# Seven products for seven of eight up-projection pieces, and adding transfers for half of the down pieces, in a streaming-encoder block

## The chip, the core and the metric

The kernel runs on one core of a Trainium2 chip. The metric is the device time of one execution in microseconds. The core's engines run side by side, each through its own list of instructions in a fixed order, and wait for one another through semaphores: TensorE (PE, matmuls and, as PEld, the loads of their stationary operand), VectorE (DVE), ScalarE (ACT), GpSimd (POOL) and SyncE (SP, which issues most transfers). Data lie in HBM, in the on-chip SBUF, and in PSUM, eight banks of 128 x 512 float32 into which TensorE writes.

## What is computed

One layer of an encoder block on 256 tokens of width 2048: a gated feed-forward, a mixing stage with two recurrences, a cross attention, a second feed-forward, and a last norm. The change touches the two feed-forwards alone:

```
D_MODEL = 2048; SEQ = 256; DEPTH = 1
D_FF = 256 * ((8 * D_MODEL // 3 + 255) // 256)      # 5632

def swiglu(h, w_up, w_down):
    gate, up = jnp.split(h @ w_up, 2, axis=-1)
    return (jax.nn.silu(gate) * up) @ w_down

x = x + 0.5 * swiglu(rms_norm(x, ffn1_norm[l]), ffn1_w_up[l], ffn1_w_down[l])
...
x = x + 0.5 * swiglu(rms_norm(x, ffn2_norm[l]), ffn2_w_up[l], ffn2_w_down[l])
```

All of it is float32.

## The kernel before

**High and low parts.** A float32 operand is split into a high part `h` (a rounded copy, made by ScalarE) and a low part `l` (the remainder, a subtraction on VectorE); `split`, L119 to L121, issues the two. A product is then three matmuls of 128 x 128 by 128 x 512: high by high, low by high, high by low (`three`, L448 to L454). The first loop of `three` issues all matmuls with the weights' high parts, the second those with their low parts.

**Pieces.** Weights come in pieces of 128 x 2048 float32, 1 MB each. The hidden width of 5632 is cut into 11 groups of 512 columns. The up-projection of one group takes eight pieces, p = 0 to 7; a piece holds two blocks of 128 rows of the gate half and of the up half, that is four 128 x 512 blocks, and multiplies a pair of blocks of the activations, for two halves of 128 tokens. That is a 2 x 2 by 2 x 2 block product. It is done in one of three ways, by the table `PRODUCTS`:

- "plain" (first group): 8 products, 24 matmuls.
- "fast": 7 products, 21 matmuls. It is a seven-product scheme which needs differences of weight blocks. `prepare` (L195 to L222) makes them: `td`, four 512-wide blocks by three VectorE instructions (L213 to L215), and then splits 1536 columns of the piece into `h` and `l` and the differences, in two halves, into `th` and `tl`. It also needs sums of activation blocks, which `operand_pairs` makes ahead ("sums", into the second half of the slots `xh` and `xl`).
- "mixed": 8 products, 24 matmuls, that add into the same seven accumulators as the fast ones. It needs the weights' plain `h` and `l` alone, but two differences of activation blocks ("less"), 256 columns.

In the second and third group (g = 1, 2) even p are mixed and odd p fast. From the fourth on (g = 3 to 10) p = 0 and p = 6 are mixed, the six others fast, in the order 1, 3, 0, 4, 2, 6, 5, 7. The seven accumulators take seven of the eight PSUM banks. After the last piece of a group they are combined (`e0` to `e3`, L535 to L547), made into the hidden activations (`activate`, L483 and L484) and, some pieces later, turned by TensorE (`turn`, L491 to L496).

**Down pieces.** The down-projection of a block of 512 hidden columns has four pieces (c = 0 to 3), each 24 matmuls (`three`, for two halves of tokens), all plain. From g = 3 on four down pieces follow every group; the down pieces of two blocks are worked off over two groups, so that c takes one pair of accumulators for two pieces, and after the second the residual is updated (L563). `ffn_order` (L42 to L58) writes the whole order.

**Adding transfers.** `prepare` has a second way to make the low part, the kind "added" (`begin_added`, L186 to L193): the piece is loaded into `own`, a pool of one buffer; ScalarE writes its negative, rounded, into `l`; then a transfer issued by POOL adds `own` to `l`, so that VectorE has no part in it. `prepare` later lets ScalarE write `h` from `own`. This is begun one piece ahead of the others. In the kernel before, both mixed pieces of every group from the fourth on are "added", except p = 0 of the fourth group, which is plain: 15 pieces per feed-forward.

**Order on the engines.** `weights` prepares one piece ahead of the piece that is multiplied. What of this stands where on each engine is then settled by the framework's scheduler when the program is built; the instructions of neighbouring pieces interleave. Buffers: three each for `raw`, `h`, `l`, and for "wide", which holds `td`, `tl` and the combination buffer `ev`; 24 slots of 1024 columns for activations.

**Sums of activations.** In `operand_pairs` the list `BOTH` names the pairs which need both "less" (for the second and third group) and "sums" (from the fourth on): 2 and 4. Their "less" lies in a slot `xd` of its own, two pairs wide; for the other even pairs it lies in the second half of `xh` and `xl`. In the first feed-forward the sums of pairs 2 and 4 are made when pieces 17 and 18 of the plan (counted from 0) are prepared, by the dictionary `rest`.

Of the kernel before, what the change touches and what calls it, by code (L numbers as in the profile page):

```python
# [9 lines left out]
F32R = mybir.dt.float32r  # L10
# [3 lines left out]
P = 128  # L14
# [5 lines left out]
NG = DFF // 512  # L20
# [21 lines left out]
def ffn_order():  # L42

    out, down = [("plain", 0, p) for p in range(8)], [("down", 0, 1, c, 0) for c in range(4)]
    for g in range(1, NG):
        if g < 3:  # L50
            out += [(("mixed", "fast")[p % 2], g, p) for p in (0, 1, 2, 3, 5, 4, 7, 6)]
        else:
            out += [("mixed" if p in (0, 6) else "fast", g, p) for p in (1, 3, 0, 4, 2, 6, 5, 7)]
        if g > 2 and g % 2:
            down = [("down", g - 2, 2, c, b) for c in range(4) for b in (g - 2, g - 1)]
        n = 2 if g < 3 else 4
        out, down = out + down[:n], down[n:]
    return out + [("down", NG - 2, 2, c, b) for c in range(4) for b in (NG - 2, NG - 1)]  # L58
# [3 lines left out]
def block_kernel(ctx: ExitStack, tc: tile.TileContext, xT, xin, memT, vec, gfin, bgate, lruw, wu1, wd1, win, wv,  # L62
# [14 lines left out]
    scoped = {}  # L77

    @contextmanager
    def scope(**pools):  # L80
        with ExitStack() as inner:
            for name, bufs in pools.items():
                scoped[name] = inner.enter_context(tc.tile_pool(name=name, bufs=bufs, reuse_waits="tile"))
            yield
            scoped.clear()

    def slot(dt=F32, name="slot"):
        return slots.tile([P, 1024], dt, name=name, tag="slot")
# [12 lines left out]
    def col(name, i=0, n=1):  # L101
        a = VEC[name][0] + i
        return vt[:, a:a + n]
# [15 lines left out]
    def split(h, l, raw):  # L119
        done["high"] = act.activation(h, raw, ACT.Copy).ins  # L120
        dve.tensor_tensor(out=l, in0=raw, in1=h.bitcast(F32), op=ALU.subtract)  # L121
# [4 lines left out]

    plan, ahead = [], []
    orders = dict.fromkeys(("ffn1", "ffn2"), ffn_order())

    def plan_ffn(name, wu, wd):  # L130
        for e in orders[name]:
            src = wd[e[4], e[3]] if e[0] == "down" else wu[e[1], e[2]]
            kind = "fast" if e[0] == "fast" else "added" if e[0] == "mixed" and e[1:] > (3, 0) else "plain"
            plan.append(((name,) + e, src, kind))

    def plan_columns(name, w, which):
# [2 lines left out]
    def plan_rows(name, w, g):  # L139
        plan.extend(((name, g, kq), w[g, kq], "plain") for kq in range(w.shape[1]))  # L140

    plan_ffn("ffn1", wu1, wd1)
    for hf in range(2):
        for base in (8, 0):
# [11 lines left out]
    for name, w in (("mv", wvm), ("o", wo)):  # L156
        for g in range(4):
            plan_rows(name, w, g)
    plan_ffn("ffn2", wu2, wd2)

    head, rest = [], {}
# [175 lines left out]
            return r  # L337


    FFN_POOLS = dict(wide=3, own=1)  # L340

    class TokenSquares:

# [58 lines left out]

    BOTH = [2, 4]
    xd = []

    def operand_pairs(src, gain, q, xg, out):

        for a in src:  # L410
            i = len(out)
            g = xg[:, i * 512:(i + 1) * 512]
            for z in range(2):
                act.activation(g[:, z * T:][:, :T], a[:, z * T:(z + 1) * T], ACT.Copy,
                               scale=col(gain, 4 * q + 2 * i + z))
            h, l = slot(F32R, "xh"), slot(F32R, "xl")
            split(h[:, :512], l[:, :512], g)
            less = None if i else (h[:, 512:768], l[:, 512:768])
            if 2 * q + i in BOTH:
                if 2 * q + i == BOTH[0]:  # L420
                    xd.append(slot(F32R, "xd"))
                n = 512 * BOTH.index(2 * q + i)
                less = [xd[-1][:, a:a + 256] for a in (n, n + 256)]
            out.append(((h, l), less))

        def sums(which=((0, "less"), (0, "sums"), (1, "less"), (1, "sums"))):
            s = slot(name="xs")
            for i, ((h, l), less) in enumerate(out):
                a = [xg[:, i * 512 + j * P:][:, :P] for j in range(4)]

                def made(h, l, n, at, terms):
                    o = [s[:, at + j * P:][:, :P] for j in range(n)]
                    for j, (x, y, op) in enumerate(terms(o)):
                        dve.tensor_tensor(out=o[j], in0=x, in1=y, op=op)
                    split(h, l, s[:, at:at + n * P])

                if less and (i, "less") in which:
                    made(*less, 2, 0, lambda o: ((a[0], a[1], ALU.subtract), (a[2], a[3], ALU.subtract)))
                if (i or 2 * q in BOTH) and (i, "sums") in which:
                    if not i and len(which) > 1:  # L440
                        s = slot(name="xs")
                    made(h[:, 512:], l[:, 512:], 4, 512 * i,
                         lambda o: ((a[1], a[3], ALU.add), (o[0], a[0], ALU.subtract),
                                    (a[1], a[0], ALU.subtract), (a[2], o[1], ALU.subtract)))

        return sums
# [130 lines left out]
    def head_x(p):  # L577

        q = p // 2
        if p % 2 == 0:  # L580
            xq[q] = slot(name="xf"), slot(name="xg"), []
        src, xg, out = xq[q]
        a = p % 2 * 512
        sp.dma_start(src[:, a:a + 512], xT[:, p * 512:(p + 1) * 512])
        sums = operand_pairs([src[:, a:a + 512]], "ffn1_norm", q, xg, out)
        if p % 2:
            sums1.append(sums)
        pairs1.append(out[-1])
# [19 lines left out]
    made = rest[7], rest[8]  # L608
    rest[7] = lambda: [f() for f in (lambda: head_residual(3), made[0])]
    rest[8] = lambda: [f() for f in (head_rstd, made[1])]  # L610
    for q, i in ((1, 17), (2, 18)):
        rest[i] = lambda q=q: sums1[q](((0, "sums"),))


# [48 lines left out]

    with scope(**FFN_POOLS):
        ffn("ffn1", pairs1, sq1, to_mix, rstds=rstd1)
# [390 lines left out]
    def to_ffn(c):  # L1056
        out = []
        sums2.append(operand_pairs(turned(xt[c]), "ffn2_norm", c, slot(name="xg"), out))
        pairs2.extend(out)
        if c < 2:  # L1060
            sums2.pop(0)()
# [34 lines left out]

    with scope(**FFN_POOLS):
        ffn("ffn2", pairs2, sq4, to_out, late, sums2)
# [93 lines left out]
```

## Time and profile before

| | |
|---|---|
| time, median of 3 runs | 2442.7 us (2442.57 to 2443.22) |
| profiled execution, its own time | 2442.24 us |
| its span, first to last instruction | 2440.5 us |
| mean granted TensorE clock | 0.999 |
| DMA | 507.59 MB, mean 208 GB/s |

How to read it: "busy" is the time that an engine spends in instructions; for a matmul the end is modelled, so matmuls of 0.39 us each that begin 0.23 us apart overlap. A row of a group gives line, engine, operation, tile written, tiles read, shape, count, then busy time and mean nanoseconds of one, then the idle time of the engine before them and what ended it. A row of a timeline gives start and length in microseconds. A row of the waits gives engine and line, what it waited for, the total in us, how often, and the longest. A row of stretches gives from and to, length, busy time (and instructions) of PE, PEld, DVE, ACT and POOL, the granted clock, the busy share of the 16 DMA engines and GB/s.

### The profile page before, as it was taken

How to read it: one execution, taken by the hardware profiler on the slowest of the kernel's cores; microseconds unless marked ns; L12 is line 12 of the kernel's file. 1: busy time of each engine (PE TensorE's matmuls, PEld its weight loads, DVE VectorE, ACT ScalarE, POOL GpSimd, SP SyncE). 2: the span in 40 equal slices, each digit the busy share in tenths (PEclk: the TensorE clock that was granted, in tenths of full speed). 3: DMA queues.
4: the chain of work that ended last, by engine and by line, in shares of the span. 5: the costliest groups of instructions: out<-in, count | busy, mean ns of one | idle time of the engine just before them, and what ended most of it. 6: DMA issues, size and time to landing. Idle time of an engine off the chain costs nothing.

```text
span 2440.5 us, 30183 instructions
## 1 busy us (share of the span) xinstructions
PE 2430.0 (100%) x12250; PEld 2033.8 (83%) x12250; DVE 1892.8 (78%) x2016; ACT 1390.8 (57%) x1398; POOL 28.3 (1%) x36
## 2 busy tenths in 40 slices
PE   9999999999999999999999999999999999999998
PEld 8888888888888888888888888888888888888887
DVE  6999999999765757577565676556589999999995
ACT  8566666666554454477435554555555666666664
POOL 0000000000000000000000000000000000000000
PEclk9999999999999999999999999999999999999999
DMA  8557777677555545445555555544555677777763
GB/s 296 207 204 243 255 234 236 234 241 239 200 181 192 180 173 179 176 171 217 191 189 186 206 196 190 190 173 155 189 191 185 232 238 234 234 239 241 237 216 151
DMA packets 75020, 507.59 MB, mean 208 GB/s; under 512 B 8320, under 2 KB 8576, under 8 KB 15232
## 3 DMA queue, kind: packets, MB, share of 16 engines
q1 hardware_dynamic: 69840, 473.06, 53.3%
q0 software_dynamic: 4320, 31.46, 6.7%
q8 instruction: 96, 1.57, 0.2%
q10 hardware_dynamic: 720, 1.13, 0.1%
q14 instruction: 44, 0.36, 0.0%
HBM read 472.07 MB, written 2.10 MB: 194 GB/s over the span
## 4 chain that ended last, share of the span: by engine, by line
PE 97%; DVE 1%; ACT 1%; DMA 1%; issue 0%; SPq 0%; ACTq 0%; DVEq 0%
PE acc L451 18%; PE acc L454 18%; PE acc L452 18%; PE acc L231 11%; PE acc L252 8%; PE acc L253 8%; PE acc L255 8%; PE acc L235 6%; PE acc L491 1%; PE acc L391 1%; ACT h L120 0%; PE acc L768 0%; DVE l L121 0%; DMA xf<-xT 0%; PE acc L1051 0%; PE acc L1006 0%
## 5 line engine op out<-in xcount | busy, mean ns | idle before, releaser
L121 DVE TENSOR_TENSOR l<-raw,h 128x2048 fp32r<-128x2048 f32 (+2 forms) x422 | 877.9, 2087 | 364.8 <-ACT h L120 354.7
L120 ACT ACTIVATE h<-raw 128x2048 fp32r<-128x2048 f32 (+2 forms) x422 | 736.7, 1752 | 615.1 <-PE acc L253 206.2
L451 PE MATMUL acc<-h,xh 128*128 128x512 f32 x1280 | 499.0, 391 | 0.4 <-ACT h L120 0.3
L452 PE MATMUL acc<-h,xl 128*128 128x512 f32 x1280 | 496.9, 389 | 0.0
L120 ACT ACTIVATE h<-td 128x1024 fp32r<-128x1024 f32 x224 | 229.7, 1056 | 177.0 <-PE acc L452 130.8
L252 PE MATMUL acc<-h,ops 128*128 128x512 f32 x832 | 326.9, 393 | 0.0
L253 PE MATMUL acc<-h,ops 128*128 128x512 f32 x832 | 324.3, 390 | 0.0
L121 DVE TENSOR_TENSOR tl<-td,h 128x1024 fp32r<-128x1024 f32 x224 | 267.4, 1220 | 31.6 <-ACT h L120 29.0
L451 PEld LDWEIGHTS acc<-h,xh 128*128 128x128 f32 x1280 | 240.3, 188 | 53.2 <-ACT h L120 3.4
L452 PEld LDWEIGHTS acc<-h,xl 128*128 128x128 f32 x1280 | 240.3, 188 | 49.4
L231 PE MATMUL acc<-ops,h 128*128 128x512 f32 x1152 | 277.9, 393 | 0.2
L451 PE MATMUL acc<-h,hidop 128*128 128x512 f32 x704 | 275.7, 392 | 0.0
L452 PE MATMUL acc<-h,hidop 128*128 128x512 f32 x704 | 274.3, 390 | 0.0
L231 PEld LDWEIGHTS acc<-ops,h 128*128 128x128 f32 x1152 | 211.9, 188 | 42.8 <-DVE ops L292 0.9
L454 PE MATMUL acc<-l,xh 128*128 128x512 f32 x832 | 218.3, 389 | 0.0
L255 PE MATMUL acc<-l,ops 128*128 128x512 f32 x832 | 206.1, 390 | 0.0
L454 PE MATMUL acc<-l,hidop 128*128 128x512 f32 x704 | 188.3, 389 | 0.0
L255 PEld LDWEIGHTS acc<-l,ops 128*128 128x128 f32 x832 | 156.2, 188 | 32.4
L454 PEld LDWEIGHTS acc<-l,xh 128*128 128x128 f32 x832 | 156.0, 188 | 32.5
L252 PEld LDWEIGHTS acc<-h,ops 128*128 128x128 f32 x832 | 156.3, 188 | 32.3
L253 PEld LDWEIGHTS acc<-h,ops 128*128 128x128 f32 x832 | 156.3, 188 | 31.6
L454 PEld LDWEIGHTS acc<-l,hidop 128*128 128x128 f32 x704 | 132.2, 188 | 27.5
(220 smaller groups left out, 2347.9 us busy)
## 6 DMA issues: line engine op xcount, KB each, us to landing
raw<-wu SPq DMA_DIRECT2D x142, 1024.0 KB, 4.8
raw<-wd SPq DMA_DIRECT2D x88, 1024.0 KB, 4.8
raw<-win SPq DMA_DIRECT2D x40, 1024.0 KB, 4.8
raw<-wg SPq DMA_DIRECT2D x32, 1024.0 KB, 4.8
own<-wu SPq DMA_DIRECT2D x30, 1024.0 KB, 5.4
l<-own POOLq DMA_DIRECT2D x30, 1024.0 KB, 7.7
raw<-wab SPq DMA_DIRECT2D x16, 1024.0 KB, 4.8
raw<-wout SPq DMA_DIRECT2D x16, 1024.0 KB, 4.8
```

The costliest lines, as they stand in the source:

```text
L120: done["high"] = act.activation(h, raw, ACT.Copy).ins
L121: dve.tensor_tensor(out=l, in0=raw, in1=h.bitcast(F32), op=ALU.subtract)
L231: pe.matmul(acc, h[:, k * P:(k + 1) * P], xs[k], start=k == 0, stop=False)
L235: done["product"] = pe.matmul(acc[:, :T], l[:, k * P:(k + 1) * P], xs[k][:, :T], start=False, stop=k == KT - 1).ins
L252: pe.matmul(accs[t], x[:, t * P:][:, :P], h[j], start=first and j == 0, stop=False)
L253: pe.matmul(accs[t], x[:, T + t * P:][:, :P], h[j], start=False, stop=False)
L255: done["product"] = pe.matmul(accs[t], x[:, t * P:][:, :P], l[j], start=False, stop=last and j == 3).ins
L391: pe.transpose(accs[m // 2][:, m % 2 * T + t * P:][:, :P], tile[:, t * 512 + m * P:][:, :P], ident)
L451: pe.matmul(acc, ah, bh, start=start, stop=False)
L452: pe.matmul(acc, al, bh, start=False, stop=False)
L454: pe.matmul(acc, ah, bl, start=False, stop=stop)
L491: pe.transpose(acc[:, z * T + t * P:][:, :P], hid[t][:, (2 * y + z) * P:][:, :P], ident)
```

## The change

From the fourth group on p = 0 becomes fast, so that only p = 6 is mixed, and the order of the pieces becomes 1, 3, 0, 6, 4, 2, 5, 7. The kind "added" now goes to the mixed piece of every group from the fourth on, that of the fourth included, and to every second down piece of the blocks 1 to 8: two of the four that follow each group from g = 3 to g = 10, the first and the fourth of them. `BOTH` gains pair 0. As `xd` has room for two, the "less" of the third pair (4) is put in a buffer of a new pool `third` of 512 columns, made when it is first written. In the first feed-forward the sums of pairs 0, 2 and 4 are made at pieces 22, 23 and 24 of the plan.

```diff
@@ ffn_order
         else:
-            out += [("mixed" if p in (0, 6) else "fast", g, p) for p in (1, 3, 0, 4, 2, 6, 5, 7)]
+            out += [("mixed" if p == 6 else "fast", g, p) for p in (1, 3, 0, 6, 4, 2, 5, 7)]
@@ plan_ffn
-            kind = "fast" if e[0] == "fast" else "added" if e[0] == "mixed" and e[1:] > (3, 0) else "plain"
+            kind = "fast" if e[0] == "fast" else "plain"
+            if e[0] == "mixed" and e[1] > 2:
+                kind = "added"
+            if e[0] == "down" and 0 < e[1] < NG - 2 and (e[3] + e[4] - e[1]) % 2 == 0:
+                kind = "added"
@@
-    FFN_POOLS = dict(wide=3, own=1)
+    FFN_POOLS = dict(wide=3, own=1, third=1)
@@ operand_pairs
-    BOTH = [2, 4]
+    BOTH = [0, 2, 4]
...
-                less = [xd[-1][:, a:a + 256] for a in (n, n + 256)]
+                less = [xd[-1][:, a:a + 256] for a in (n, n + 256)] if n < 1024 else []
...
+                if less == [] and (i, "less") in which:
+                    third = scoped["third"].tile([P, 512], F32R, name="xd", tag="xd")
+                    less.extend((third[:, :256], third[:, 256:]))
@@
-    for q, i in ((1, 17), (2, 18)):
+    for q, i in ((0, 22), (1, 23), (2, 24)):
         rest[i] = lambda q=q: sums1[q](((0, "sums"),))
```

## The prediction

> **What bounds the kernel now.** I read the page's head first, then the waits of TensorE, then busy time by stretch, and last the order of single instructions inside one group.
>
> ```profile
> span 2440.5 us, 30183 instructions
> PE 2430.0 (100%) x12250; PEld 2033.8 (83%) x12250; DVE 1892.8 (78%) x2016; ACT 1390.8 (57%) x1398; POOL 28.3 (1%) x36
> ```
> ```profile
> PE warm L109 <- DVE ones L106: 1.1, 1, 1.1
> PE acc L451 <- ACT h L120: 0.3, 1, 0.3
> ```
> TensorE (PE) is busy all the span and waits 1.4 us in total. Its busy time is modelled, so the second view is needed: nothing holds it up. The two feed-forward stages are therefore as long as their list of matmuls. What could take over is seen by stretch (PE, weight loads, DVE, ACT, POOL, then clock, DMA share, GB/s):
>
> ```profile
> 110.00:172.00 62.00, 62.00 (x282) 51.02 (x281) 60.75 (x59) 35.62 (x31) 0.00 (x0) 1.00 0.51 187
> 1840.00:1902.00 62.00, 62.00 (x282) 50.98 (x281) 57.69 (x56) 36.50 (x31) 0.00 (x0) 1.00 0.54 190
> 2011.40:2073.50 62.10, 62.10 (x279) 51.52 (x278) 57.37 (x56) 38.36 (x32) 1.76 (x2) 1.00 0.72 237
> ```
> The last row is one whole period of a group from the fourth on: PE 62.10 of 62.10, VectorE (DVE) 57.37, so 4.73 us of DVE are free. In the third group of the first feed-forward DVE is at 60.75 of 62.00: there it is nearly the second bound. The granted clock is 1.00 in all three.
>
> **What is removed: 48 matmuls.** In the order of PE's instructions the pieces of one group begin at
>
> ```profile
> 345.67 0.39 PE L451 MATMUL acc<-h,xh 128*128 128x512 f32 x1
> 349.52 1.07 PE L454 MATMUL acc<-tl,xh 128*128 128x512 f32 x4
> 350.43 0.39 PE L451 MATMUL acc<-h,xh 128*128 128x512 f32 x1
> 355.19 0.39 PE L451 MATMUL acc<-h,xh 128*128 128x512 f32 x1
> 360.63 0.39 PE L451 MATMUL acc<-h,xh 128*128 128x512 f32 x1
> ```
> Two "fast" pieces of 7x3 matmuls take 4.76 us each, the "mixed" piece of 8x3 takes 5.44: 0.227 us a matmul. Groups 3 to 10 of two feed-forwards turn one piece each: 16 x 0.68 = 10.9 us. The path it lies on is PE's own, without cover. More than that cannot be gained, since PE waits for nothing that could go away; a period becomes 62.10 - 0.68 = 61.42 us.
>
> **What it adds on DVE.**
>
> ```profile
> 348.74 2.36 DVE L121 TENSOR_TENSOR tl<-td,h 128x1024 fp32r<-128x1024 f32 x2
> 351.01 1.22 DVE L213 TENSOR_TENSOR td<-raw 128x1024 f32<-128x1024 f32 x1
> 357.54 1.22 DVE L213 TENSOR_TENSOR td<-raw 128x1024 f32<-128x1024 f32 x1
> 365.61 1.22 DVE L213 TENSOR_TENSOR td<-raw 128x1024 f32<-128x1024 f32 x1
> 378.29 2.36 DVE L121 TENSOR_TENSOR tl<-td,h 128x1024 fp32r<-128x1024 f32 x2 [0.98 <-ACT h L120]
> 383.86 4.49 DVE L121 TENSOR_TENSOR l<-raw,h 128x2048 fp32r<-128x2048 f32 x2 [0.53 <-ACT h L120]
> 388.27 0.68 DVE L536 TENSOR_TENSOR ev<-acc,ev 128x512 f32<-128x512 f32 x1
> ```
> A fast piece costs DVE 357.54 - 351.01 = 6.53 us; the low part of a plain down piece (388.27 - 383.86)/2 = 2.20. Per group: +6.53 - 2 x 2.20 = +2.13, so 59.50 of 61.42 us. As a throughput it still fits, with 1.9 us free, hidden behind PE.
>
> **Does it fit in order?** The new order 1 3 0 | 6 | 4 2 5 7 has runs of three and four fast pieces, each of which takes DVE 1.8 us longer than PE. With p=1 at 0, PE starts 3 at 4.76, 0 at 9.52, 6 at 14.28, 4 at 19.72, 2 at 24.48, 5 at 29.24, 7 at 34.00 and ends at 38.76. A fast piece needs its second half of `tl` 19 matmuls in (its first was at 349.52 - 345.67 = 3.85), at 4.30. DVE today begins the third fast piece at 351.01 - 345.67 = 5.34. Five fast pieces in one go (0 4 2 5 7) end at 5.34 + 5 x 6.53 = 37.99; piece 7 needs it at 38.30. The others have 1.9 to 5 us. So the order fits with 0.3 us to spare, if DVE is never held up; the free 1.9 us lie in the downs behind, where DVE catches up. I take nothing per steady group. The other end is from today's last two fast pieces, which took from 365.61 to 380.65, 15.04 us, with waits for ScalarE in between. Since `td` of piece 5 needs a "wide" buffer that piece 4 frees at 24.48, about 0.2 later it starts, and 24.7 + 15.0 = 39.7 is 1.4 us late. Those waits came from buffers that PE frees, and with DVE behind instead of ahead they should be gone.
>
> **The fourth group (g=3) pays a transition.** It takes over DVE from the saturated groups:
>
> ```profile
> 93.18 0.69 DVE L536 TENSOR_TENSOR ev<-acc,ev 128x512 f32<-128x512 f32 x1 [0.22 <-PE acc L454]
> 159.76 1.23 DVE L121 TENSOR_TENSOR tl<-td,h 128x1024 fp32r<-128x1024 f32 x1 [0.92 <-ACT h L120]
> 194.69 2.28 DVE L121 TENSOR_TENSOR l<-raw,h 128x2048 fp32r<-128x2048 f32 x1
> 196.89 1.22 DVE L121 TENSOR_TENSOR tl<-td,h 128x1024 fp32r<-128x1024 f32 x1
> ```
> ```profile
> 198.34 0.39 PE L451 MATMUL acc<-h,hidop 128*128 128x512 f32 x1
> 198.57 0.61 PE L454 MATMUL acc<-tl,xh 128*128 128x512 f32 x2
> ```
> ```profile
> L434 DVE TENSOR_TENSOR xs<-xg 128x128 f32<-128x128 f32 x40 | 9.5, 284 | 0.0
> L121 DVE TENSOR_TENSOR xl<-xs,xh 128x512 fp32r<-128x512 f32 x12 | 8.1, 684 | 0.7 <-ACT xh L120 0.7
> ```
> Piece 7's last `tl` ends at 198.11, just ahead of its matmuls at 198.57, and a down matmul already stands before them. After the change p=0, plain today, is fast (+6.53 - 2.20), the down piece's 2.20 at 194.69 falls away, and PE is there 0.68 earlier: 6.53 - 2.20 - 2.20 + 0.68 = 2.8 us late. The third operand sum costs DVE 4 x 0.284 + 0.684 = 1.8 us in each feed-forward; in the second it lies in a stretch that PE fills anyway, in the first DVE has only 0.22 + 0.92 idle from 93 to 160, so 0.7 are added. Both together: 0 to 2.8 + 3.5 = 6.3 us. The sums also move from the 18th and 19th to the 23rd to 25th prepared piece. By then 24 slots are taken (16 `xh`/`xl`, `xd`, 3 `xg`, 4 of hidden operands), so they may have to wait for the downs that end near 158; two sums of 1.8 then fall into g=3 and the end is 9.9. The low end is nothing, as the products of 6 or of the first down can stand ahead of the late ones, as the row at 198.34 does today. I take 2.4, nearer to today's row, which lost PE nothing, than to the ledger.
>
> **ScalarE, transfers and SyncE.**
>
> ```profile
> L191 ACT ACTIVATE l<-own 128x2048 fp32r<-128x2048 f32 x30 | 57.3, 1910 | 13.8 <-DMA own<-wu 13.8
> L200 ACT ACTIVATE h<-own 128x2048 fp32r<-128x2048 f32 x30 | 57.1, 1904 | 1.2 <-PE acc L452 1.2
> L120 ACT ACTIVATE h<-raw 128x1536 fp32r<-128x1536 f32 x112 | 166.9, 1490 | 159.6 <-issue 94.8 <-PE acc L452 62.9 <-ACT hidop L495 1.6
> L120 ACT ACTIVATE h<-td 128x1024 fp32r<-128x1024 f32 x224 | 229.7, 1056 | 177.0 <-PE acc L452 130.8 <-DVE td L213 20.4 <-DVE td L215 15.2
> ```
> ```profile
> 356.30 1.92 ACT L191 ACTIVATE l<-own 128x2048 fp32r<-128x2048 f32 x1 [0.45 <-DMA own<-wu]
> 358.58 0.86 POOL L192 DMA_DIRECT2D l<-own  x1 [15.83 <-ACT l L191]
> ```
> ```profile
> DMA to landing us min/median/max: 7.0/7.7/11.6
> SPq L190 <- DMA l<-own: 29.6, 9, 4.9
> own<-wu SPq DMA_DIRECT2D x30, 1024.0 KB, 5.4
> ```
> ScalarE gains a fast piece (1.49 + 2 x 1.06) and two extra passes of 1.91, and loses 3.81: 38.4 + 3.6 = 42 of 61.4 us, hidden. Adding transfers rise from 2 to 3 a group; one costs (0.72 - 0.54)/2 of a period's DMA share, so the share goes to about 0.82, hidden. Their latency is what counts. From ScalarE's pass to the landed low part it is 2.28 + 7.7 = 10.0 us. D1 needs it 1.8 us into itself, at 40.6; its `l` buffer comes free at about 23.6 to 30, so it lands at 34 to 40. The single `own` buffer is refilled only after that transfer has landed (the SyncE row), and SyncE's later loads of the third down and of the next group's first pieces queue behind; these have 3 us and more. So D4's chain is 39 + 0.3 + 5.4 + 10.0 = 54.7 against 55.1 + 1.8 = 56.9: 2.2 us to spare, and -1.7 where a transfer takes 11.6. I take nothing. The Trainium skill (SBUF — State Buffer, Who interferes with whom) says that a VectorE instruction with two SBUF inputs locks out a GpSimd instruction that reads SBUF until it ends. By that rule each issue could stand 2.3 us longer, and D4's margin would be gone. The trace agrees less: the issue at 358.58 followed ScalarE's end at 358.22 by 0.36 us with DVE 92% busy on such instructions.
>
> **The sum.** On the profiled execution, 2442.24 us (span 2440.5 and 1.74 around it): -10.9 + 2.4 = 2433.7. The runs' median, 2442.7, lies 0.5 above it: 2434.2.
>
> **Rivals.** (a) All of it arrives: the matmuls of other pieces cover g=3 wholly; for it speaks that PE lost nothing in today's g=3. 2442.7 - 10.9 = 2431.8. (b) Adding transfers late at D4: for it the chain with 2.2 us to spare and the 11.6 us landing, against it that none of the 30 held PE up. At 0.4 us in 16 groups, 6.4 us on top of the forecast: 2440.6. (c) Slower: the run 4 2 5 7 keeps today's waits and piece 7 is 1.4 us late in each of 16 groups, 22 us in place of the 2.4: 2442.7 - 10.9 + 22.4 = 2454.2; from 0.68 us a group on it eats the gain. For it: 0.3 us of margin; against: PE's matmuls are already interleaved across pieces where `tl` is late. That 48 matmuls do not go is excluded by the two tables of products.
>
> **Chances.** Forecast 0.50 (own range 2431.8 to 2437.5), (a) 0.20, (b) 0.13, (c) 0.17. A measurement tells 0.2%, 4.9 us, from no change. Forecast and (a) are faster, 0.70; (b) is the same, 0.13; (c) slower, 0.17. The range runs from (a) with a little spread, 2431, to 2449, in the middle of (c), where about 0.12 is left above.
>
> **What would show it.** PE's count falls by 48 to 12202; a period of 61.4 us with PE full; DVE near 59.5; three POOL issues a group; in g=3 waits of PE for `tl`, or matmuls of the first down among those of piece 7. Wrong would be: PE waiting for `tl` of piece 7 in every group (c), or for the low part of a down piece behind POOL (b), or a period under 61.4.

## The result and the profile after

The changed kernel takes 2449.4 us (median of 7 runs, 2448.86 to 2452.64) against 2442.6 us for the kernel before in the same session (2441.6 to 2443.22): a ratio of 1.0032 with an interval of 1.002 to 1.0044, slower by 6.8 us. The profiled execution took 2449.4 us, with a span of 2447.6. The forecast was 2434.2.

The page's head, then TensorE's waits, then the largest wait of TensorE's weight loads (line 458 is the high matmuls of `three`, 461 its low ones, 120 and 121 the two halves of `split`, 196 the adding transfer):

```profile
span 2447.6 us, 30240 instructions
PE 2429.0 (99%) x12202; PEld 2019.5 (83%) x12202; DVE 1912.8 (78%) x2088; ACT 1448.6 (59%) x1450; POOL 43.9 (2%) x54
```
```profile
PE acc L461 <- DMA l<-own: 4.2, 2, 2.9
PE acc L458 <- ACT h L120: 1.3, 4, 0.6
PE acc L461 <- DVE l L121: 1.3, 1, 1.3
```
```profile
PEld acc L458 <- ACT h L120: 17.3, 51, 1.0
```

The 48 matmuls are gone (12250 to 12202), and TensorE now waits: three times in the fourth groups and just behind them (4.2 and 1.3 us), and in the last row 51 times for a high part that ScalarE writes. The weight load goes ahead of its matmul, so it is there that most of this wait is booked. By stretch, with the columns as in the prediction:

```profile
110.00:172.00 62.00, 61.93 (x278) 50.09 (x276) 62.00 (x73) 38.73 (x35) 1.00 (x1) 1.00 0.59 199
172.00:217.00 45.00, 40.83 (x178) 32.95 (x178) 39.33 (x39) 29.95 (x24) 1.72 (x2) 1.00 0.72 234
441.64:503.67 62.03, 61.85 (x276) 50.56 (x276) 58.62 (x60) 41.75 (x34) 2.59 (x3) 1.00 0.80 254
```

In the first row VectorE is full, 62.00 of 62.00 (60.75 before). In the second, the last part of the fourth group and the downs behind it, TensorE has 4.2 us without work. The third is a steady group: nearly three matmuls' time above 61.42 us, with VectorE at 58.62.

Where the time goes is read by taking the start of the combination's first ScalarE copy, once per group, as a clock (us):

| end of group | before | after | difference |
|---|---|---|---|
| first feed-forward, g=2 | 140.47 | 140.95 | +0.5 |
| g=4 | 261.36 | 266.23 | +4.9 |
| g=10 | 633.92 | 638.73 | +4.8 |
| second feed-forward, g=1 | 1821.58 | 1827.34 | +5.8 |
| g=4 | 1993.28 | 1999.74 | +6.5 |
| g=10 | 2365.84 | 2372.03 | +6.2 |

From g=4 to g=10 the difference falls by 0.1 and 0.3 us, where six groups of 0.68 should have won 4.1 each: 4.0 + 3.8 = 7.8 us lost in steady groups, 0.6 to 0.7 each. The rest, 7.1 us in the span + 10.9 - 7.8 = 10.2 us, is lost around the two fourth groups and in the entry and exit of the stages.

**A steady group.** TensorE, ScalarE and VectorE near the end of one (order 1 3 0 6 4 2 5 7; the second half of piece 5's `th` is at stake):

```profile
445.31 0.61 PE L461 MATMUL acc<-l,xh 128*128 128x512 f32 x2
446.10 0.50 PE L458 MATMUL acc<-h,xh 128*128 128x512 f32 x1 [0.18 <-ACT h L120]
446.44 0.40 PE L459 MATMUL acc<-h,xl 128*128 128x512 f32 x1
```
```profile
442.66 1.06 ACT L120 ACTIVATE h<-td 128x1024 fp32r<-128x1024 f32 x1 [1.42 <-DVE td L217]
443.63 1.47 ACT L120 ACTIVATE h<-raw 128x1536 fp32r<-128x1536 f32 x1
445.00 1.04 ACT L120 ACTIVATE h<-td 128x1024 fp32r<-128x1024 f32 x1
```
```profile
438.52 1.76 DVE L121 TENSOR_TENSOR l<-raw,h 128x1536 fp32r<-128x1536 f32 x1 [0.63 <-ACT h L120]
440.19 1.22 DVE L121 TENSOR_TENSOR tl<-td,h 128x1024 fp32r<-128x1024 f32 x1
441.33 1.22 DVE L217 TENSOR_TENSOR td<-raw 128x1024 f32<-128x1024 f32 x1
443.31 0.69 DVE L219 TENSOR_TENSOR td<-raw,td 128x512 f32<-128x512 f32 x1
```

Two matmuls from 445.31 end the supply at 445.76; the next starts at 446.10, 0.34 late, and its successor comes 0.34 instead of 0.227 later: 0.45 us. It needed a half that ScalarE wrote from 445.00 to 446.04. VectorE's differences for it were ready at 444.00, but ScalarE's list had piece 7's 1.47 us ahead of it; and VectorE had begun piece 5's differences only at 441.33, after a wait for ScalarE and that piece's own 1.76 us of low part. ScalarE's pass before that low part had waited too. Here, and in the same pass of the next group:

```profile
436.99 1.49 ACT L120 ACTIVATE h<-raw 128x1536 fp32r<-128x1536 f32 x1 [0.85 <-DMA raw<-wu]
```
```profile
499.03 1.49 ACT L120 ACTIVATE h<-raw 128x1536 fp32r<-128x1536 f32 x1 [0.75 <-PE acc L459]
```

The first row is the exception. In two of the twelve steady groups the pass waits for a load that SyncE issued late, behind a refill of `own` that had to wait for an adding transfer of 11.5 or 11.6 us. In the ten others it waits until a high matmul of TensorE has freed an `h` buffer; from there to the late half it is 9.1 us (499.03 to 508.14), and the gap is 0.24 + 0.11 us. `tl`, on which the prediction's ledger was made, is late without harm: TensorE works on the next down piece meanwhile.

**The fourth group** (TensorE, then POOL, ScalarE and SyncE's queue):

```profile
173.31 0.98 PE L461 MATMUL acc<-l,xh 128*128 128x512 f32 x3 [1.25 <-DVE l L121]
204.33 0.73 PE L461 MATMUL acc<-l,hidop 128*128 128x512 f32 x2 [2.92 <-DMA l<-own]
```
```profile
193.51 0.86 POOL L196 DMA_DIRECT2D l<-own  x1 [29.33 <-ACT l L195]
```
```profile
191.30 1.90 ACT L195 ACTIVATE l<-own 128x2048 fp32r<-128x2048 f32 x1
```
```profile
204.34 0.33 SPq L194 DMA_DIRECT2D own<-wd  x1
```

VectorE, full since before 172, gives TensorE a low part 1.25 us late; the first down's adding transfer is issued at 193.51 and has landed only when SyncE's queue moves on, at 204.3.

### The profile page after: what moved, and what is told of

The parts are those of the page before. It is cut to its first block, busy times and chain, and to the rows that moved or that the text cites. A ratio compares the mean times of both kernels' runs of the same rounds, so it can differ in the third digit from the quotient of the medians.

```text
span 2447.6 us, 30240 instructions
## 1 busy us (share of the span) xinstructions
PE 2429.0 (99%) x12202; PEld 2019.5 (83%) x12202; DVE 1912.8 (78%) x2088; ACT 1448.6 (59%) x1450; POOL 43.9 (2%) x54
## 4 chain that ended last, share of the span: by engine, by line
PE 81%; DVE 8%; DMA 5%; ACT 3%; issue 3%; SPq 0%; ACTq 0%; POOLq 0%; DVEq 0%
PE acc L458 13%; PE acc L459 13%; PE acc L461 12%; PE acc L235 11%; PE acc L256 8%; PE acc L257 8%; PE acc L259 8%; PE acc L239 6%; DMA l<-own 3%; DVE l L121 3%; ACT h L120 3%; DVE tl L121 2%; DVE td L217 2%; DMA own<-wd 1%; PE acc L498 1%
## 5 line engine op out<-in xcount | busy, mean ns | idle before, releaser
L121 DVE TENSOR_TENSOR l<-raw,h 128x2048 fp32r<-128x2048 f32 (+2 forms) x404 | 828.9, 2055 | 346.6 <-ACT h L120 346.2
L120 ACT ACTIVATE h<-raw 128x2048 fp32r<-128x2048 f32 (+2 forms) x404 | 696.4, 1727 | 501.3 <-PE acc L257 207.0
L458 PE MATMUL acc<-h,xh 128*128 128x512 f32 x1256 | 491.2, 393 | 2.4 <-ACT h L120 1.3
L459 PE MATMUL acc<-h,xl 128*128 128x512 f32 x1256 | 486.0, 390 | 0.0
L120 ACT ACTIVATE h<-td 128x1024 fp32r<-128x1024 f32 x256 | 266.9, 1054 | 217.4 <-PE acc L459 90.6
L121 DVE TENSOR_TENSOR tl<-td,h 128x1024 fp32r<-128x1024 f32 x256 | 309.1, 1218 | 18.6 <-ACT h L120 18.4
L461 PE MATMUL acc<-l,xh 128*128 128x512 f32 x744 | 200.1, 389 | 1.3 <-DVE l L121 1.3
L461 PEld LDWEIGHTS acc<-l,xh 128*128 128x128 f32 x744 | 139.5, 188 | 30.9 <-DVE l L121 1.7
```

The lines of the kernel that those rows point to most:

```text
L458: pe.matmul(acc, ah, bh, start=start, stop=False)
L459: pe.matmul(acc, al, bh, start=False, stop=False)
L461: pe.matmul(acc, ah, bl, start=False, stop=stop)
```

## The experiments

Ratios are to runs of the kernel before on the same chip, whose medians lay between 2442.1 and 2442.5 us.

**1. Is the loss in the fourth group, and is the steady loss VectorE's load?** The first kernel begins the change at the fifth group. The second keeps p=0 mixed, so that VectorE is relieved, but leaves the order and the change's transfers; the low part of p=0, which a transfer makes in the kernel before, is made by VectorE.

```diff
 e1: change from the fifth group on
-            out += [("mixed" if p == 6 else "fast", g, p) for p in (1, 3, 0, 6, 4, 2, 5, 7)]
+            first = (1, 3, 0, 4, 2, 6, 5, 7) if g == 3 else (1, 3, 0, 6, 4, 2, 5, 7)
+            out += [("mixed" if p == 6 or (g, p) == (3, 0) else "fast", g, p) for p in first]
-            if e[0] == "mixed" and e[1] > 2:
+            if e[0] == "mixed" and e[1:] > (3, 0):
-            if e[0] == "down" and 0 < e[1] < NG - 2 and ...
+            if e[0] == "down" and (1, 1) < (e[1], e[3]) and e[1] < NG - 2 and ...
-    for q, i in ((0, 22), (1, 23), (2, 24)):
+    for q, i in ((1, 17), (2, 18), (0, 37)):
 e2: p=0 mixed, made by split
-... ("mixed" if p == 6 else "fast", g, p)
+... ("mixed" if p in (0, 6) else "fast", g, p)
-            if e[0] == "mixed" and e[1] > 2:
+            if e[0] == "mixed" and e[1] > 2 and e[2] == 6:
-    BOTH = [0, 2, 4]
+    BOTH = [2, 4]
```


> The change begins with the fifth group instead of the fourth; the fourth keeps the old order, its old pieces and plain downs, and the third sum is made while the downs behind it run. Theory (VectorE's backlog): the fourth group takes over a saturated VectorE and cannot carry a seventh fast piece, so the 6.5 us of PE gaps in the first feed-forward and 3.7 in the second up to the start of the fifth group fall to 3 or less in all, and the time to 2441 to 2444; the 0.5 us gap per later group stays. Rival (the transfers of the first down block land late wherever they begin): the gaps move by one group, 2449 to 2451.

> Undoes the seven products for p=0 alone (mixed, with plain high and low parts); order 1 3 0 6 4 2 5 7, the transfer for the mixed p=6 of the fourth group too, and the two transfers per group for the downs stay. Theory (VectorE): VectorE falls from 58.6 to about 54.6 us of a period and PE has no gaps, 2441.5 to 2443.5, as before the change. Rival (the adding transfers delay PE by themselves): the gaps of 2.9 and 1.3 us behind a transfer and some of the steady ones stay, 2446 or more.

The first: 2443.4 us, ratio 1.0005 (0.9996 to 1.0014). 6 of the 6.8 us come back, the waits of the fourth group are gone, and the steady groups stay at 62.0 to 62.4. The second: 2448.1, 1.0025 (1.0015 to 1.0034), not the 2442 that VectorE's load as a cause asked for. A gap stands, now in piece 7, although VectorE has 7.7 us of the period free:

```profile
441.00:503.48 62.48, 62.39 (x280) 51.48 (x279) 54.78 (x55) 40.15 (x33) 2.59 (x3) 1.00 0.80 253
```

The chain of waits through one such run (start, length, engine, tile and line):

```profile
431.14 0.03 ACTq L120
431.21 1.07 ACT h L120
432.30 0.98 DVE tl L121
...
434.67 1.72 DVE l L121
436.39 1.15 DVE td L217
...
440.11 1.13 DVE td L217
...
442.98 1.67 DVE l L121
444.65 0.61 DVE td L219
...
445.29 1.07 ACT h L120
446.36 0.04 issue
446.40 0.50 PE acc L458
```

It begins where TensorE frees an `h` buffer (431.14), goes through `th` and `tl` of piece 2, then all of 5 and 7, and ends in the last `th` half, 15.3 us later; TensorE's own work between the two points is 0.36 us shorter (the gap of 0.25 and the slow restart of 0.11). The tail of the run 4 2 5 7 thus cannot be prepared in the time that TensorE takes for it, however idle VectorE was before: it cannot start earlier, for want of a buffer.

**2. Order alone, transfers alone, downs alone.**

```diff
 e5: as e2, and the downs plain
-            if e[0] == "down" and 0 < e[1] < NG - 2 and ...
+            if e[0] == "down" and NG < e[1] < NG - 2 and ...
 e6: as e2, in the old order
-... for p in (1, 3, 0, 6, 4, 2, 5, 7)]
+... for p in (1, 3, 0, 4, 2, 6, 5, 7)]
 e12: the whole change, but the downs plain (the edit of e5 alone)
```


> The old products (p=0 and p=6 mixed, p=0 plain), no transfers for the downs, only the order 1 3 0 6 4 2 5 7 and the transfer for p=6 of the fourth group left of the change. Theory (order): the run 4 2 5 7 begins from a th that waits for the h buffer which piece 4 frees, and its last th half is 0.25 us late, whatever VectorE has to do; the gap of 0.36 us a group of the run with p=0 mixed stays, 2447 to 2450. Rival (the transfers for the downs are the cause there): no gap, 2442 to 2443.

> The old products and the old order 1 3 0 4 2 6 5 7 (p=0 mixed and plain), with the adding transfers for p=6 and for two downs per group. Theory (order): no gap, 2441.5 to 2443. Rival (transfers): a gap of about 0.36 us a group, 2446 to 2449.

> Seven products for seven pieces, but all downs plain, so that the mixed p=6 alone has its low part from a transfer. Theory: VectorE has 58.6 + 4.4 = 63 us of work in a group that PE does in 61.4, so VectorE sets the period, 63.5 to 65, and the time is 2470 to 2500. Rival (VectorE's work does not bind, PE and the transfers do): 2445 to 2455.

In e5 and e6, as in e2, VectorE makes the low part of p=0, so "alone" holds but for that and for the transfer of p=6 in the fourth group. Order alone: 2452.3, 1.0041 (1.0026 to 1.0056); the gap is at the same place as in e2 with the same 0.25 and 0.11, and one more beside it. So the order makes a gap without the seventh fast piece and without the downs' transfers; the comparison that changes nothing but the order follows in 8. Transfers alone were to be free and were not: 2452.4, 1.0043 (1.0028 to 1.0058), with waits for the low part of plain downs (4.8 us in seven). With all downs plain: 2456.2, 1.0057 (1.0043 to 1.0071), far below the 2470 or more that I expected from VectorE's count. A stretch of it:

```profile
440.00:502.80 62.80, 62.59 (x276) 50.53 (x275) 62.09 (x62) 38.91 (x33) 0.86 (x1) 1.00 0.63 217
```

Now VectorE is nearly full, 62.09 of 62.80, and TensorE waits for its low parts, 2.5 us in nine. The two transfers per group are worth about 0.75 us in the whole change (62.8 against 62.07 on average).

**3. Symptoms in the fourth group.** The downs of the first block pair made plain; the third sum made early.

```diff
 e3
-            if e[0] == "down" and 0 < e[1] < NG - 2 and ...
+            if e[0] == "down" and 1 < e[1] < NG - 2 and ...
 e11
-    for q, i in ((0, 22), (1, 23), (2, 24)):
+    for q, i in ((1, 17), (2, 18), (0, 19)):
```


> The down pieces of the first such block pair, which follow the fourth and fifth group, are plain again (8 transfers less in all, 2.2 us of VectorE more for each). Theory (VectorE's backlog in the fourth group): the late transfer was only where the backlog showed; with 4.4 us more on VectorE in each of these groups the gaps grow, 2450 to 2455. Rival (the transfer itself is what is late there): the gaps of 2.9 and 1.3 us go and nothing comes in their place, 2445.

> The whole change, but the three sums of the first feed-forward are made at pieces 17, 18 and 19 of the plan, two of them where they were before. Theory (VectorE is saturated all the way from the second group to the fourth, so it does not matter where in it they stand): 2448 to 2451. Rival (the move of the sums into the third group's pieces causes the backlog of the first feed-forward): its loss in the fourth group falls by 3 us or more, 2446 or less.

2452.5, 1.0043 (1.0028 to 1.0058), and 2452.2, 1.0041 (1.0026 to 1.0056): no better than the change, whose own runs reach 2452.6. Neither the late transfer nor the place of the sums was the root; in e3 TensorE waits 3.5 us for other transfers, the first of those that are left, and 1.8 us for VectorE's low parts.

**4. The halves that are needed first, made first.** In `prepare` the split of `raw` is put behind the two of `td`.

```diff
         h, l = split_tiles()
-        split(h[:, 512:], l[:, 512:], raw[:, 512:])
         th = hp.tile(...)
...
             split(th[:, a:a + 1024], tl[:, a:a + 1024], td[:, a:a + 1024])
+        split(h[:, 512:], l[:, 512:], raw[:, 512:])
```


> In a fast piece the split of the 1536 raw columns is put behind that of the differences, so that the scheduler favours td, th and tl before l. Theory (VectorE's order in the run 4 2 5 7: l of piece 5 stands before its td, so its second th half is late): the steady gap of 0.5 us shrinks, 0.2 to 0.5 in 14 groups, 2442 to 2446. Rival (VectorE's throughput with its waits for h buffers sets the period, whatever the order): 2448 to 2452.

2530.5, 1.0356 (1.0335 to 1.0376): both theories missed by 80 us. Its waits:

```profile
PE acc L461 <- DMA l<-own: 50.6, 19, 5.4
```

The same instructions in another order hold TensorE up 50.6 us behind adding transfers alone. A second part of the loss is the clock, the third last figure of this stretch:

```profile
364.80:368.20 3.40, 3.40 (x10) 2.66 (x9) 1.91 (x3) 0.23 (x1) 0.00 (x0) 0.50 0.81 340
```

Ten such stretches, 44.2 us together, have a granted clock of 0.50 or 0.51; that is worth about 21 us (an estimate: half of the 41.8 us that TensorE is busy in them). Which instruction came to stand where was not followed further.

**5. Shorter runs, more buffers.** The mixed piece one place later makes the runs four and three, counted to the mixed piece: 1 3 0 4, then 2 5 7. And a fourth `h` buffer, paid for with two of the 24 slots.

```diff
 e7
-... for p in (1, 3, 0, 6, 4, 2, 5, 7)]
+... for p in (1, 3, 0, 4, 6, 2, 5, 7)]
 e8
-    hp = pool("h", 3)
+    hp = pool("h", 4)
-    slots = pool("slots", 24)
+    slots = pool("slots", 22)
```


> The whole change, but with the mixed piece one place later: 1 3 0 4 6 2 5 7, runs of four and three. Theory (a run of four fast pieces that starts from a PE-freed h buffer is a quarter of a microsecond too long): the gap goes from piece 5 or 7 to piece 4 and keeps its size, as 4 is now the fourth in a row; the first run also carries the residual and turning work of VectorE, so 2449 to 2455. Rival (only VectorE's total over the group counts): as the change, 2449.

> The whole change with four h buffers instead of three; the room comes from two of the 24 activation slots. Theory (the h buffer that PE frees starts the late chain): the steady gap of 0.35 to 0.5 us a group goes, the period falls from 62.05 to 61.4 to 61.6, and the time to 2438 to 2444, if the missing slots cost nothing before the fourth group. Rival (VectorE at 95% of the period is the limit): the period stays 62.0, 2448 or more.

The first takes 2451.8, 1.0039 (1.0024 to 1.0054), in the range that the theory gave, but not for its reason. Its steady groups:

```profile
440.60:502.30 61.70, 61.70 (x277) 50.74 (x276) 58.33 (x60) 41.72 (x34) 2.59 (x3) 1.00 0.80 257
```

No gap is left: the groups take 61.60 to 61.70 us, and VectorE has as much to do as in the change. So it is not any run of four that is too long: 2 5 7 behind the mixed piece is in time, and so is 1 3 0 4, which begins behind the downs. The time was lost in the fourth groups, +8.2 us by the end of g=4 in the first feed-forward; about 3 us of e7's whole loss are two stretches of 3.4 us there at a granted clock of 0.50 (an estimate: half of the 6.3 us that TensorE is busy in them).

With four `h` buffers: 2445.9, 1.0014 (1.0005 to 1.0024). The steady groups fall to 61.9 us on average, not to the 61.4 to 61.6 expected, and in seven of the twelve TensorE still waits for a high half, now in piece 7:

```profile
452.01 0.50 PE L458 MATMUL acc<-h,xh 128*128 128x512 f32 x1 [0.15 <-ACT h L120]
```

VectorE works almost without a pause from 431.1 to 450.6 there, so its list is what the half waits for, with 1.9 us of ScalarE for an `own` piece in front. The fourth buffer moves the start of the chain and does not remove the gap; that the freed `h` buffer starts it in the change is read from the change's own rows. The fourth group's loss stays. Two slots fewer may cost by themselves, which was not tried alone.

**6. Both remedies at once, at the fifth group.**

```diff
 e9: e1 with the order of e7
-            first = (1, 3, 0, 4, 2, 6, 5, 7) if g == 3 else (1, 3, 0, 6, 4, 2, 5, 7)
+            first = (1, 3, 0, 4, 2, 6, 5, 7) if g == 3 else (1, 3, 0, 4, 6, 2, 5, 7)
 e10: e1 with the old order throughout
-... for p in first]
+... for p in (1, 3, 0, 4, 2, 6, 5, 7)]
```


> Both remedies: the change begins with the fifth group, and from there the order is 1 3 0 4 6 2 5 7. Theory (two separate losses, the fourth group's backlog and the gap in the run 4 2 5 7): they add up, 14 groups save 0.45 us each on top of the run that begins with the fifth group, 2436 to 2438.5. Rival (the group in which the change begins always pays 4 to 8 us in this order, as it did from the fourth on): 2441 to 2446.

> As the run before, but the order stays that of the kernel before, 1 3 0 4 2 6 5 7, so five fast pieces, the mixed one, two. Theory (what counts is how many fast pieces follow the last th that waits for PE behind the mixed piece): two behind it are safer than three, and VectorE enters the first run with the slack of the downs, so the gap stays away, 2436 to 2439. Rival (a run of more than four is too long for VectorE wherever it lies): gaps in piece 4 or 2, 2442 or more.

The first: 2442.6, 1.0001 (0.9992 to 1.001), where 2436 to 2438.5 was expected. The second: 2463.4, 1.0086 (1.0072 to 1.01): with five fast pieces in a row TensorE waits 8.4 us for `h`. The first's steady groups take 61.6 to 61.7 us, but the period behind its first changed group takes 66.6, 5 us more. Lines stand one lower in these runs (462 for 461, 122 for 121, 197 for 196); L491 and L492 are the two instructions of `activate`, on ScalarE and VectorE. In time order, POOL, SyncE's queue, ScalarE, VectorE, TensorE:

```profile
251.52 0.86 POOL L197 DMA_DIRECT2D l<-own  x1 [16.92 <-ACT l L196]
```
```profile
263.16 0.33 SPq L195 DMA_DIRECT2D own<-wd  x1
```
```profile
268.09 1.92 ACT L196 ACTIVATE l<-own 128x2048 fp32r<-128x2048 f32 x1 [6.65 <-DMA own<-wd]
...
274.13 0.70 ACT L491 ACTIVATE ev<-ev,rtok 128x512 f32<-128x512 f32 x1
```
```profile
274.87 0.75 DVE L492 SCALAR_TENSOR_TENSOR ev<-ev,rtok 128x512 f32<-128x512 f32 x1 [1.66 <-ACT ev L491]
275.54 2.28 DVE L122 TENSOR_TENSOR l<-raw,h 128x2048 fp32r<-128x2048 f32 x1
```
```profile
277.88 1.19 PE L462 MATMUL acc<-l,hidop 128*128 128x512 f32 x4 [3.08 <-DVE l L122]
```

Read backwards: TensorE waits for a plain down's low part, which stands in VectorE's list behind the activation of L492; that waits for ScalarE's L491, which stands in ScalarE's list behind the next adding piece's first pass; that waits 6.65 us for the load into `own`, which SyncE could issue only at 263.16, because the one `own` buffer was in use until the transfer of 251.52 had landed, 11.6 us after its issue. A transfer for a down piece that needs nothing of VectorE has so delayed a down piece that does.

**7. Where it starts.** The order of e7, begun at different places.

```diff
 e13: in the second feed-forward alone, from its fifth group
+    orders = {"ffn1": ffn_order(NG), "ffn2": ffn_order(4)}
 e14: as e9, the downs of blocks 1 and 2 plain
-            if e[0] == "down" and (1, 1) < (e[1], e[3]) and e[1] < NG - 2 and ...
+            if e[0] == "down" and (2, 9) < (e[1], e[3]) and e[1] < NG - 2 and ...
 e15: from the sixth group in both, downs as in e14
+            first = (1, 3, 0, 4, 2, 6, 5, 7) if g < 5 else (1, 3, 0, 4, 6, 2, 5, 7)
+            out += [("mixed" if p == 6 or p == 0 and g < 5 else "fast", g, p) for p in first]
 e16: in the second alone, from its sixth group, downs as in e14
 e18: from the seventh group in both (g < 6), downs from (3, 1) < (e[1], e[3]) on: e9 moved by two groups
```


> The first feed-forward is as before the change (six fast pieces, its old order, plain downs); the second has seven products for seven pieces, three adding transfers and the order 1 3 0 4 6 2 5 7 from its fifth group on, as in the run with the fifth group and four-then-three order in both. Theory (the first feed-forward's first changed group takes back what its six steady groups win, the second's does not): the first ends as before, the second gains 6 or 7 groups of 0.43 us and pays 0.7 at its first: 2442.3 - 2.5 = 2439.8, between 2438.5 and 2441. Rival (the second's cheap start came from what the first had shifted): a start of 4 us in the second too, 2442 to 2445.

> As the run with the fifth group and four-then-three order, but the down pieces before and behind the fourth and fifth groups (blocks 1 and 2) stay plain; adding transfers serve downs from block 3 on. Theory (the 3.1 us wait in the first changed group is a plain down's low part that VectorE's list sets behind instructions which wait for ScalarE, and ScalarE is held up by the first transfers' passes): the wait goes, VectorE gets 2 x 2.2 us more in one group, and the time is 2439 to 2441. Rival (VectorE is simply behind there and 4.4 us more load make it worse): the wait grows to 5 to 8 us, 2444 to 2450.

> As the run with the fifth group and four-then-three order, but a group later in both feed-forwards: groups 4 and 5 stay as before, downs from block 3 on have the transfers. Theory (the price is one of taking over VectorE while it is still catching up behind the third group; a group later it has caught up): a start of 0 to 1 us in each feed-forward, 2 x 6 groups x 0.43 won: 2442.3 - 5.2 + 1 = 2438, between 2437 and 2440. Rival (any first changed group in the first feed-forward pays, because its order on VectorE is settled by where the pieces change kind): 4 us or more again, 2441 to 2444.

> The second feed-forward alone, from its sixth group on, four-then-three. Theory (one start of at most 1 us, six groups of 0.43): 2442.3 - 2.6 + 0.5 = 2440.2, between 2439.5 and 2441. Rival (a start of 3 us or more): 2442 to 2445.

> The run of the fifth group with four-then-three order moved by two groups, so that the switch stands at the same place of the two-group cycle of the down pieces, at the seventh group. Theory (the switch at the fifth group pays because VectorE is still catching up there): no price, 10 groups of 0.43: 2442.2 - 4.3 + 1 = 2439, between 2437 and 2440. Rival (it pays because of its place in the two-group cycle of the downs): 3 to 4 us at the start of each or of the first feed-forward: 2441 to 2446.

| | us | ratio (interval) |
|---|---|---|
| e13, second alone, fifth | 2440.3 | 0.9992 (0.9983 to 1.0001) |
| e14, fifth, downs later | 2450.3 | 1.0034 (1.0021 to 1.0046) |
| e15, sixth | 2436.7 | 0.9978 (0.9969 to 0.9987) |
| e16, second alone, sixth | 2439.3 | 0.9988 (0.998 to 0.9997) |
| e18, seventh | 2438.6 | 0.9985 (0.9976 to 0.9994) |

The sixth group is the best place: 5.4 us faster than the kernel before and 12.7 faster than the change. Its page, TensorE's waits (this row is all of them) and a steady group:

```profile
PE 2424.8 (100%) x12214; PEld 2023.8 (83%) x12214; DVE 1906.6 (78%) x2074; ACT 1431.0 (59%) x1436; POOL 38.7 (2%) x48
```
```profile
PE warm L110 <- DVE ones L107: 1.1, 1, 1.1
```
```profile
441.64:503.30 61.66, 61.66 (x277) 50.60 (x276) 58.24 (x60) 41.59 (x35) 2.61 (x3) 1.00 0.81 256
```

36 matmuls fewer, 8.2 us, of which 5.4 arrive: 12 groups at 61.65 instead of 61.42 account for 2.8. In the group above that rest has no single place: some two dozen steps from one matmul to the next are 0.23 to 0.28 us long, where the kernel before has three. Half of it comes from the second feed-forward (e16, 2.8 us). The seventh group has the fifth's place in the two-group cycle of the downs; its 30 matmuls, 6.8 us, less ten groups of 0.23 leave 4.5, of which 3.7 arrive, so it pays at most 0.9 at its start, and the place in the cycle is not what the fifth pays for. The chain of e9 in e15, one group later:

```profile
313.13 0.87 POOL L197 DMA_DIRECT2D l<-own  x1 [21.35 <-ACT l L196]
```
```profile
322.22 0.33 SPq L195 DMA_DIRECT2D own<-wd  x1
```
```profile
327.05 1.92 ACT L196 ACTIVATE l<-own 128x2048 fp32r<-128x2048 f32 x1 [3.32 <-DMA own<-wd]
```

Here the transfer landed after 9.1 us, not 11.6, ScalarE stood 3.3 us, and TensorE did not wait. e14 shows the wait of e9 again, in both feed-forwards: 2.8 and 3.9 us for plain downs behind L492, with ScalarE waiting 8.1 us for `own` before the second. The chain is shown; why one transfer takes 9 and another nearly 12 us, and whether VectorE's backlog has a part in it, is not.

**8. Order and start, apart.** e15 with the change's own order.

```diff
-            first = (1, 3, 0, 4, 2, 6, 5, 7) if g < 5 else (1, 3, 0, 4, 6, 2, 5, 7)
+            first = (1, 3, 0, 4, 2, 6, 5, 7) if g < 5 else (1, 3, 0, 6, 4, 2, 5, 7)
```


> As the run from the sixth group, but with the change's own order 1 3 0 6 4 2 5 7 from there on. Theory (the start and the run of four are two losses that add): no start's price, but each of the 12 groups stands at 62.05 us in place of 61.63 with the small gap at piece 5 or 7 back: 2436.7 + 12 x 0.42 = 2441.7, between 2440.5 and 2443. Rival (the small gap was a late effect of the backlog from the fourth group and goes with it): periods of 61.6, 2436 to 2438.

2442.1, 0.9999 (0.999 to 1.0008), as the theory said. Its steady groups take 62.05 us, and TensorE's weight loads wait as in the change:

```profile
PEld acc L459 <- ACT h L121: 16.3, 47, 1.2
```

So the gap belongs to the order, not to the early start. All of the two factors (us against the kernel before):

| first changed group | order 1 3 0 6 4 2 5 7 | order 1 3 0 4 6 2 5 7 |
|---|---|---|
| fourth | +6.8 (the change) | +9.3 (e7) |
| fifth | +1.1 (e1) | +0.3 (e9) |
| sixth | -0.1 (e17) | -5.4 (e15) |
| seventh | not run | -3.7 (e18) |

The two factors do not simply add: the second order wins 5.3 us at the sixth group and 0.8 at the fifth. At the fourth it is 2.5 us behind, about as much as e7 loses at the half clock, so that row does not rank the orders.

## Why the prediction was wrong, by its steps

**What bounds the kernel, and the 48 matmuls: right.** The count fell to 12202, and a kernel that keeps TensorE fed gets most of the saving (e15: 61.65 us a group, forecast 61.42).

**"Does it fit in order?" failed.** The step read "the order fits with 0.3 us to spare ... I take nothing per steady group". Measured were 62.07 us on average, 0.65 a group above 61.42 and 7.8 us in all; 0.4 of the 0.65 belongs to the order (e15 against e17), the rest is there in the other order too. The step counted VectorE's time from `td` to `tl` as if the five pieces ran without a break, and dropped its own other end, that the run waits for buffers TensorE frees, because those waits "should be gone" with VectorE busier. They were not: the chain of waits begins at a freed `h` buffer in ten of the change's twelve steady groups, and in e2, with VectorE 7.7 us free, as well. The deadline was the wrong one too: not piece 7's `tl`, which TensorE can put off, but the second `th` half, which the high matmuls need first. This is near to rival (c), in which the run 4 2 5 7 keeps its waits, with another operand late and the price mis-sized: 0.65 us a group, not 1.4, so just under the 0.68 at which the sign would turn, and alone it makes the change break even (e17, -0.1 us).

**The fourth group failed in size.** The term was 2.4 us from a bound of 0 to 9.9; 10.2 us were lost outside the steady groups. Beginning a group later, with the order kept, takes 6 us back (e1). I took the row in which TensorE had lost nothing before as the nearer one, although the row of the third group had VectorE at 60.75 of 62.00; it went to 62.00 of 62.00. Its sign is due to this term: with the steady loss alone the change was level, with both it is slower.

**VectorE, ScalarE, transfers.** The loads came near: VectorE 58.6 (59.5 forecast), ScalarE 41.75 (42), DMA share 0.80 (0.82) of a period. "I take nothing" for the transfers held in ten of the change's twelve steady groups, where two have a load late behind a transfer, and failed in its fourth groups, where the rows show 4.2 us of waits; taking those first transfers away made it no better (e3). The chain through the one `own` buffer, rival (b), was the right place with the right trigger (a transfer of 11.6 us), but it hit through the lists of ScalarE and VectorE, on another down piece than the one reckoned (e9).

The rows for POOL's issue and the landing of its transfers, in the change:

```profile
L196 POOL DMA_DIRECT2D l<-own x48: 859/866/1002, 163.2 to 2376.6; - x48
```
```profile
DMA to landing us min/median/max: 7.4/8.2/12.7
```

The prediction put up to 2.3 us on an issue by a rule of the Trainium skill (SBUF — State Buffer, Who interferes with whom), and carried it too far: the page has a VectorE instruction with two SBUF inputs contend with a GpSimd instruction that reads SBUF, not with one that only writes it, and says that its probe saw `tensor_copy` hold up a DMA but not `tensor_tensor`, which is most of what VectorE does here. The trace agrees: with VectorE busy for 58.6 of the 62.0 us of a steady group, the 48 issues took 0.86 us at the median and 1.00 at most.

## What to carry to other kernels

A busy share with room in it does not say that a run of hard pieces fits: follow the run from the buffer that lets it start to the operand that is needed first, engine by engine, and compare with the bound engine's time between those two points. Put the relief (here the mixed piece) where it shortens the run that starts from a freed buffer, and try a change that loads a second engine from a later place than right behind a stretch in which that engine is full; from the sixth group on the order was worth 5 us here, and the later start 7 to 15, each as much as the saving that was kept, or more. That VectorE's backlog is why the early start costs so much is likely and not shown. When a transfer relieves an engine, look also at the in-order lists in which its helper instructions now wait, since what stands behind them pays.

## What the runs showed beyond that

After a gap the first matmul is followed by the next only 0.34 us later, where the pitch is 0.227: a gap of 0.3 us costs 0.4. The landing of the same 1 MB adding transfer was spread from 7.4 to 12.7 us with three a group (7.0 to 11.6 with two). Their number does not decide it: with one a group it is 7.9 us at the median in e12 and 13.0 in e5, whose row is

```profile
DMA to landing us min/median/max: 7.4/13.0/14.7
```

A wait can cost more than its length: in e4, e7, e8, e10, e11 and e14 the granted clock falls to about 0.50 for 3.4 or 6.8 us, mostly during or just behind a wait of TensorE (2.1 us in e8, 5.1 in e10), while it stays at 1.00 behind the 2.9 us of the change and the 3.1 us of e9. And the order within one helper function, with not one instruction more, was worth 81 us against the change (e4), about 21 of them by the clock, far more than any operation that was added or removed.
